# A trunk layer in float32: the input projection by one level of Strassen, its result kept in DRAM

## The chip, the cores and the metric

The kernel runs on one NeuronCore of a Trainium2 chip. The metric is the device time of one execution in microseconds (us). The engines of the core work side by side, each through its own list of instructions in a fixed order: TensorE (PE; PEld is its loading of weights), VectorE (DVE), ScalarE (ACT), GpSimd (POOL) and SyncE (SP), which here issues DMAs. A tile is a buffer in SBUF; a bank is 512 float32 columns of PSUM, where matmuls put their results.

## The reference

```python
u = rms_norm(h, ln_g[i])                         # 1024 tokens x 1024
z = u @ w_in[i]                                  # 1024 x 7168
c_val, c_glu, c_gate, hq, hf, hi, hg = jnp.split(z, split_pts, axis=-1)
y_conv = conformer_conv_branch(c_val, c_glu, c_gate, ...)   # causal conv of 31 taps, LayerNorm, @ w_pw2
y_hgrn = hgrn2_branch(hq, hf, hi, hg, lbs[i], onorm_g[i])   # 8 heads, gated recurrence in chunks
h = h + concatenate([y_conv, y_hgrn]) @ w_out[i]            # 2048 x 1024
gate = sigmoid(rms_norm(h, pe_norm_g[i]) @ w_pg[i])
h = h + gate * (p[i] @ w_pp[i])
return rms_norm(h, final_g)
```

All of it is float32; the five large products are those with w_in, w_pw2, w_out, w_pg and w_pp.

## The kernel before

Every float32 operand of a large product is split exactly into a high and a low float32r part, and a product is three matmuls: high by high, high by low, low by high. `split` makes the parts: ScalarE copies the high one (L113), VectorE subtracts (L114). `prep` loads a weight block of 512 KB into one of three raw buffers of pool `wp` and splits it there.

First x is scaled by its RMS (`scale_x`), transposed and split into `uh`, `ul` (`norm_x`), each half of the tokens by itself; the projection of p (the layer embedding) is computed and put into DRAM. Then follows the z phase. `ztile` takes one block of 128 columns of w_in and gives two PSUM banks with 512 tokens each, by 48 matmuls of 512 columns (L241 to L243). `values` gives two blocks of the heads' values with tokens on partitions, by 192 matmuls of 256 columns (L263 to L265). The activations read z straight out of PSUM. ORDER says in which order the projections of head and channel group h, its convolution (C) and its recurrent head (H) are written; the scheduler of the language then orders each engine's list by priorities. A convolution is 29 taps of 128x1024 on VectorE (L452) and a LayerNorm through transposes. The last eight z tiles, of the convolution's gate, are written behind all heads (`conv_gate`).

After that come `pw` (w_pw2; 8 tiles of 48 matmuls, the gate read back from DRAM), the output projection with tokens on partitions, its first four token blocks in `oA` (all 16 row blocks of w_out in one go, with the heads' results `yhr` loaded and split between them) and the other four in `oB`, then `norm_T` and the gated layer embedding `pg` (w_pg) with the last RMSNorm.

Of the kernel before, what the change touches and what calls it, by code (L numbers as in the profile page):

```python
# [123 lines left out]

# [605 lines left out]
```

## Time and profile before

| | us |
|---|---|
| three runs, median (lowest to highest) | 1146.06 (1145.87 to 1147.56) |
| span of the profiled execution, 0.44 above that median | 1146.5 |
| PE busy | 1124.8 |
| DVE busy | 739.5 |
| ACT busy | 443.0 |
| POOL busy | 72.0 |
| first z matmul starts | 49.1 |
| first pw matmul starts | 781.7 |

An engine is busy while one of its instructions runs. Matmuls overlap, so a matmul's cost is the distance from its start to the next one's. In a timeline a row's bracket gives the idle time before it and what ended that.

### The profile page before, as it was taken

What the parts mean: (1) busy time and instruction counts of PE and PEld (TensorE: products, weight loads), DVE (VectorE), ACT (ScalarE), POOL (GpSimd) and SP (SyncE); (2) the same over time, 40 slices, a digit from 0 to 9 for tenths busy, and PEclk for the clock granted to TensorE, in tenths of its full rate; (3) what the DMA queues carried; (4) which work ended last, traced back from release to release, by engine and by line L of the source; (5) the groups of instructions that cost most, each with busy time, mean ns of one, the idle gap of its engine ahead of it and who ended that gap; (6) DMA issues with size and microseconds to landing.
All of it is one profiled execution on the core that took longest, in us unless ns stands there. A gap on an engine that the chain in (4) does not pass through costs nothing.

```text
span 1146.5 us, 17744 instructions
## 1 busy us (share of the span) xinstructions
PE 1124.8 (98%) x7408; PEld 945.6 (82%) x7408; DVE 739.5 (65%) x1145; ACT 443.0 (39%) x811; POOL 72.0 (6%) x107
## 2 busy tenths in 40 slices
PE   6999999999999999999999999999999999999997
PEld 4888978889888789788898788888888888887886
DVE  3659579998499996599993896242334325226444
ACT  4823244253354442344532632442123324126333
POOL 3100001001001010010010010000000001001000
PEclk9899999999999999999999999999999999999999
DMA  7611121211111112111111112277335632334221
GB/s 247 236 37 55 37 66 30 74 55 39 55 57 56 59 35 74 56 37 56 57 56 56 57 56 93 74 242 254 110 92 165 195 99 77 107 109 149 92 92 56
DMA packets 85715, 104.60 MB, mean 91 GB/s; under 512 B 3290, under 2 KB 65754, under 8 KB 85634
## 3 DMA queue, kind: packets, MB, share of 16 engines
q1 hardware_dynamic: 85634, 103.46, 28.1%
q8 instruction: 58, 0.95, 0.3%
q14 instruction: 23, 0.19, 0.1%
HBM read 82.48 MB, written 20.97 MB: 90 GB/s over the span
## 4 chain that ended last, share of the span: by engine, by line
PE 89%; DVE 6%; DMA 2%; ACT 1%; issue 1%; SPq 0%; POOL 0%; POOLq 0%; ACTq 0%
PE z L241 14%; PE z L242 14%; PE z L243 14%; DVE y L452 4%; PE v L264 3%; PE v L265 3%; PE v L263 3%; PE pg L683 3%; PE pg L684 3%; PE pg L682 3%; PE oA L591 3%; PE pw L243 3%; PE pw L241 3%; PE oA L589 3%; PE oA L588 3%; PE pw L242 3%
## 5 line engine op out<-in xcount | busy, mean ns | idle before, releaser
L452 DVE SCALAR_TENSOR_TENSOR y<-vpad,par,y 128x1024 f32<-128x1024 f32 x232 | 288.8, 1278 | 1.1
L682 PE MATMUL pg<-gh,hh 128*128 128x512 f32 (+1 forms) x136 | 51.4, 378 | 0.0
L683 PE MATMUL pg<-gl,hh 128*128 128x512 f32 (+1 forms) x136 | 51.4, 378 | 0.0
L684 PE MATMUL pg<-gh,hl 128*128 128x512 f32 (+1 forms) x136 | 51.3, 377 | 0.0
L519 DVE TENSOR_TENSOR vpad<-z,gl 128x512 f32<-128x512 f32 x16 | 11.0, 691 | 42.7 <-PE z L243 42.7
L263 PE MATMUL v<-wv_0h,uh 128*128 128x256 f32 x128 | 36.7, 287 | 0.0
L265 PE MATMUL v<-wv_0h,ul 128*128 128x256 f32 x128 | 36.5, 285 | 0.0
L264 PE MATMUL v<-wv_0l,uh 128*128 128x256 f32 x128 | 36.5, 285 | 0.0
L263 PE MATMUL v<-wv_1h,uh 128*128 128x256 f32 x128 | 36.2, 283 | 0.0
L264 PE MATMUL v<-wv_1l,uh 128*128 128x256 f32 x128 | 36.2, 283 | 0.0
L265 PE MATMUL v<-wv_1h,ul 128*128 128x256 f32 x128 | 36.2, 283 | 0.0
L266 ACT ACTIVATE vt<-v 128x256 f32<-128x256 f32 x32 | 12.2, 382 | 58.9 <-PE v L265 58.9
L688 DVE TENSOR_TENSOR gt<-gt,pet 128x512 f32<-128x512 f32 (+1 forms) x17 | 11.2, 661 | 36.1 <-ACT gt L687 36.1
L108 POOL TENSOR_SCALAR ro<-sso 128x8 f32<-128x8 f32 x8 | 8.4, 1054 | 389.9 <-ACT on L129 389.9
L475 DVE TENSOR_SCALAR y<-yt,mv,ry 128x128 f32<-128x128 f32 x64 | 23.5, 404 | 13.1 <-POOL ry L109 13.1
L570 DVE SCALAR_TENSOR_TENSOR sgr<-pw,par,sgr 128x512 f32<-128x512 f32 x16 | 12.0, 750 | 30.1 <-PE pw L243 30.1
L437 ACT ACTIVATE on<-o,ro 128x128 f32<-128x128 f32 x64 | 18.5, 386 | 29.0 <-POOL ro L109 29.0
L682 PEld LDWEIGHTS pg<-gh,hh 128*128 128x128 f32 x136 | 25.6, 188 | 4.7
L683 PEld LDWEIGHTS pg<-gl,hh 128*128 128x128 f32 x136 | 25.6, 188 | 4.7
L684 PEld LDWEIGHTS pg<-gh,hl 128*128 128x128 f32 x136 | 25.6, 188 | 4.5
L483 ACT ACTIVATE yc<-yn,par 128x512 f32<-128x512 f32 x16 | 12.5, 778 | 39.8 <-PE yn L482 39.8
L129 ACT ACTIVATE on<-o 128x128 f32<-128x128 f32 x64 | 16.9, 278 | 23.3 <-PE up L409 18.9
(802 smaller groups left out, 3463.6 us busy)
## 6 DMA issues: line engine op xcount, KB each, us to landing
wz<-in_w_in_dram SPq DMA_DIRECT2D x48, 512.0 KB
wo<-in_w_out_dram SPq DMA_DIRECT2D x32, 512.0 KB
xt<-in_x_dram SPq DMA_DIRECT2D x8, 512.0 KB
pe_d<-pes SPq DMA_DIRECT2D x8, 512.0 KB
wv<-in_w_in_dram SPq DMA_DIRECT2D x8, 512.0 KB
yc_d<-yc SPq DMA_DIRECT2D x8, 512.0 KB
yh_d<-sgT SPq DMA_DIRECT2D x8, 512.0 KB
sg_d<-sgc SPq DMA_DIRECT2D x8, 512.0 KB
```

Of the source, the lines that this page charges most:

```text
L241: mm(z, lhsT=wh[:, k, :], rhs=mh[hf][k], start=k == 0, stop=False)
L242: mm(z, lhsT=wh[:, k, :], rhs=ml[hf][k], start=False, stop=False)
L243: mm(z, lhsT=wl[:, k, :], rhs=mh[hf][k], start=False, stop=k == G - 1)
L263: mm(z, lhsT=uh[hf][k][:, c], rhs=wh, start=k == 0, stop=False)
L264: mm(z, lhsT=uh[hf][k][:, c], rhs=wl, start=False, stop=False)
L265: mm(z, lhsT=ul[hf][k][:, c], rhs=wh, start=False, stop=k == G - 1)
L452: nc.vector.scalar_tensor_tensor(y[j % 2], vp[:, j:j + T], pcol(g, j), y[j % 2], op0=ALU.mult, op1=ALU.add)
L588: mm(z, lhsT=mixh[hf][k][:, c], rhs=wh[j], start=first, stop=False)
L589: mm(z, lhsT=mixh[hf][k][:, c], rhs=wl[j], start=False, stop=False)
L682: mm(z, lhsT=hh[k][:, c], rhs=gh[j][k][:, o:o + w], start=k == 0, stop=False)
L683: mm(z, lhsT=hh[k][:, c], rhs=gl_[j][k][:, o:o + w], start=False, stop=False)
L684: mm(z, lhsT=hl[k][:, c], rhs=gh[j][k][:, o:o + w], start=False, stop=k == G - 1)
```

## The change

The product of the normalised input and w_in is computed by one level of Strassen's algorithm in Winograd's form. The 56 column tiles of z are taken in 28 pairs (`zpair`). The input is cut into four quarters a, b, c, d (halves of its channels by halves of the tokens), and the seven operands a, c, d and t1 to t4 are made once, from all of x (`norm_x`, `quarter`). The weights of a pair are cut into four quarters of 256 KB, four sums of them are made on VectorE, and each of the seven factors is split: ScalarE writes the negated high part into the low tile and the high part into its own, and a DMA issued by GpSimd adds the source to the low tile in place (`factor`), where VectorE subtracted. A product is 12 matmuls of 512 columns, a pair 84. Partial sums leave PSUM by copies on ScalarE and additions on VectorE, and the four quarters of z go to DRAM; `ztile` reads a column tile back when it is needed. The values are now transposed on TensorE (`head`). The normalisation in the convolution moves from VectorE to ScalarE. In the output projection `project` takes all eight token blocks through the convolution's half of w_out, then the heads' results are loaded, and then all through the other half; each half adds to the residual by itself. Pool `wp` has two buffers instead of three.

```diff
+C_VAL, C_GLU, C_GATE, H_Q, H_F, H_V, H_G = range(7)
+RAWS, TMPS = 6, 6
+AHEAD, SOON = 3000, 4000
+ORDER = "cCCcCh" + "HCHcCh" * 2 + "HCHhHH" + "gggg"
...
+        def quarter(name, k, src, sign=1.0):
+            nc.scalar.activation(xh[name][k], src, AF.Copy, scale=sign)
+            h = xh[name][k].bitcast(F32)
+            if sign == 1.0:
+                nc.vector.tensor_tensor(xl[name][k], src, h, op=ALU.subtract)
+            else:
+                nc.vector.scalar_tensor_tensor(xl[name][k], src, sign, h,
+                                               op0=ALU.mult, op1=ALU.subtract)
+        def norm_x(k):
+            q = {}
+            for n, kk, hf in (("a", k, 0), ("c", k + KH, 0), ("b", k, 1), ("d", k + KH, 1)):
+                pt = bank("t", f"u{n}{k}")
                 for b in range(4):
-                    nc.tensor.transpose(pt[:, b * P:(b + 1) * P], xs[b][:, k * P:(k + 1) * P],
-                                        ident)
-                uh[hf][k] = up.tile([P, H], F32R, tag="u", name=f"uh{hf}_{k}")
-                ul[hf][k] = up.tile([P, H], F32R, tag="u", name=f"ul{hf}_{k}")
-                nc.scalar.activation(uh[hf][k], pt, AF.Copy, scale=pcol(k, R_LN))
-                nc.vector.scalar_tensor_tensor(ul[hf][k], pt, pcol(k, R_LN),
-                                               uh[hf][k].bitcast(F32),
-                                               op0=ALU.mult, op1=ALU.subtract)
-        xs = scale_x(0)
+                    nc.tensor.transpose(pt[:, b * P:(b + 1) * P],
+                                        xs[hf * 4 + b][:, kk * P:(kk + 1) * P], ident)
+                q[n] = st.tile([P, H], F32, tag=f"uf{n}", name=f"uf{n}{k}")
+                nc.scalar.activation(q[n], pt, AF.Copy, scale=pcol(kk, R_LN))
+                if n != "b":
+                    quarter(n, k, q[n])
+            a, b, c, d = (q[n] for n in "abcd")
+            nc.vector.tensor_tensor(a, a, b, op=ALU.subtract)
+            quarter("t1", k, a)
+            nc.vector.tensor_tensor(a, a, d, op=ALU.add)
+            quarter("t2", k, a, -1.0)
+            nc.vector.tensor_tensor(b, d, b, op=ALU.subtract)
+            quarter("t3", k, b)
+            nc.vector.tensor_tensor(c, a, c, op=ALU.subtract)
+            quarter("t4", k, c)
...
+        scale_x(1)
+        layer_embedding(1)
+        for k in range(KH):
+            norm_x(k)
...
+        def factor(name, src):
+            hi = wq.tile([P, KH, P], F32R, tag="hi", name=f"w{idx}_{name}h")
+            lo = wq.tile([P, KH, P], F32R, tag="lo", name=f"w{idx}_{name}l")
+            nc.scalar.activation(lo, src, AF.Copy, scale=-1.0)
+            nc.scalar.activation(hi, src, AF.Copy)
+            nc.gpsimd.dma_start(out=lo, in_=src, accum_op=ALU.add)
+            return hi, lo
+        def add(name, x, y):
+            o = raw(name)
+            nc.vector.tensor_tensor(o, x, y, op=ALU.add)
+            return o
+        w = {}
+        for name, r, c in (("11", 0, 0), ("21", 0, 1), ("22", 1, 1), ("12", 1, 0)):
+            w[name] = raw(name)
+            nc.sync.dma_start(w[name], w_in[r * H:(r + 1) * H, (idx + c) * P:(idx + c + 1) * P]
+                              .rearrange("(k p) c -> p k c", p=P))
+        s1 = add("s1", w["21"], w["22"])
+        s2 = add("s2", s1, w["11"])
+        s4 = add("s4", s2, w["12"])
+        s3 = add("s3", w["11"], w["21"])
+        return [factor(n, t) for n, t in (("f1", w["11"]), ("f5", s1), ("f6", s2), ("f3", s4),
+                                          ("f7", s3), ("f2", w["12"]), ("f4", w["22"]))]
+    def zpair(proj, i):
+        idx = proj * G + 2 * i
+        with tc.high_priority(AHEAD):
+            fs = weights(idx)
+        def product(z, f, xn, first, last):
+            wh, wl = f
+            for k in range(KH):
+                mm(z, lhsT=wh[:, k, :], rhs=xh[xn][k], start=first and k == 0, stop=False,
+                   skip_group_check=True)
+                mm(z, lhsT=wh[:, k, :], rhs=xl[xn][k], start=False, stop=False,
+                   skip_group_check=True)
+                mm(z, lhsT=wl[:, k, :], rhs=xh[xn][k], start=False, stop=k == KH - 1,
+                   skip_group_check=True)
+        def tmp(name):
+            return wq.tile([P, H], F32, tag="tmp", bufs=TMPS, name=f"z{idx}_{name}")
+        def copy(z, name, scale=1.0):
+            t = tmp(name)
+            with tc.high_priority(SOON):
+                nc.scalar.activation(t, z, AF.Copy, scale=scale)
+            return t
+        def out(t, c, hf):
+            nc.sync.dma_start(z_d[idx + c][:, hf * H:(hf + 1) * H], t)
+        f1, f5, f6, f3, f7, f2, f4 = fs
+        za, zd, zb = bank("za", f"za{idx}"), bank("zd", f"zd{idx}"), bank("zb", f"zb{idx}")
+        product(za, f1, "a", True, False)
+        m1 = copy(za, "m1")
+        product(zd, f5, "t1", True, False)
+        p5 = copy(zd, "p5")
+        product(za, f6, "t2", False, False)
+        u2 = copy(za, "u2")
+        product(zd, f3, "d", False, True)
+        with tc.high_priority(SOON):
+            nc.vector.tensor_tensor(u2, u2, zd, op=ALU.add)
+        out(u2, 0, 1)
+        product(za, f7, "t3", False, False)
+        u3 = copy(za, "u3")
+        with tc.high_priority(SOON):
+            nc.vector.scalar_tensor_tensor(u3, u3, -1.0, p5, op0=ALU.mult, op1=ALU.subtract)
+        out(u3, 1, 1)
+        product(zb, f2, "c", True, True)
+        with tc.high_priority(SOON):
+            nc.vector.tensor_tensor(m1, m1, zb, op=ALU.add)
+        out(m1, 0, 0)
+        product(za, f4, "t4", False, True)
+        out(copy(za, "c21", -1.0), 1, 0)
...
+    def ztile(proj, m):
+        t = wk.tile([P, T], F32, tag="ld", bufs=3, name=f"ld{proj}_{m}")
+        nc.sync.dma_start(t, z_d[proj * G + m])
+        return t
...
             r = rstd_of(mv[:, :, 1], G, 1.0, f"ry{g}")
+            nmr = sml.tile([P, G], F32, tag="nmr", name=f"nmr{g}")
+            nc.gpsimd.tensor_scalar(nmr, mv[:, :, 0], -1.0, 0.0, op0=ALU.mult, op1=ALU.add)
+            nc.gpsimd.tensor_tensor(nmr, nmr, r, op=ALU.mult)
...
+        zv = ztile(H_V, h)
+        vt = wk.tile([P, G, P], F32, tag="vt", name=f"vt{h}")
+        for hf in range(2):
+            pt = bank("t", f"v{h}_{hf}")
+            for c in range(4):
+                cc = hf * 4 + c
+                nc.tensor.transpose(pt[:, c * P:(c + 1) * P], zv[:, cc * P:(cc + 1) * P], ident)
+            nc.scalar.activation(vt[:, hf * 4:hf * 4 + 4, :],
+                                 pt.rearrange("p (c v) -> p c v", c=4), AF.Copy)
...
+    zx.close()
+    pz = ctx.enter_context(tc.tile_pool(name="pz2", bufs=1, space=PSUM, reuse_waits="tile"))
+    wp = ctx.enter_context(tc.tile_pool(name="wp", bufs=2, reuse_waits="tile"))
+    up = ctx.enter_context(tc.tile_pool(name="up2", bufs=32, reuse_waits="tile"))
     yp = ctx.enter_context(tc.tile_pool(name="yp", bufs=32, reuse_waits="tile"))
...
-        nc.sync.dma_start(sg, sg_d[m])
+        nc.sync.dma_start(sg, z_d[C_GATE * G + m])
+        nc.scalar.activation(sg, sg, AF.Silu)
...
+    def project(src_h, src_l, row0, hf, j, flip):
+        zs = [bank("z", f"o{row0}_{hf}_{j}_{b}") for b in range(4)]
+        kks = range(G // 2)[::-1 if flip else 1]
+        for n, kk in enumerate(kks):
+            wh, wl = prep(w_out[row0 + kk * 2 * P:row0 + (kk + 1) * 2 * P, j * H:(j + 1) * H]
+                          .rearrange("(k p) c -> p k c", p=P), [P, 2, H], f"wo{row0}_{hf}_{j}_{kk}")
+            for i in range(2):
+                k = 2 * kk + i
+                first, last = n == 0 and i == 0, n == G // 2 - 1 and i == 1
+                for b, z in enumerate(zs):
+                    c = slice(b * P, (b + 1) * P)
+                    mm(z, lhsT=src_h[hf][k][:, c], rhs=wh[:, i, :], start=first, stop=False)
+                    mm(z, lhsT=src_h[hf][k][:, c], rhs=wl[:, i, :], start=False, stop=False)
+                    mm(z, lhsT=src_l[hf][k][:, c], rhs=wh[:, i, :], start=False, stop=last)
+        for b, z in enumerate(zs):
+            h = halves(hs[hf * 4 + b])[j]
+            nc.vector.tensor_tensor(h, z, h, op=ALU.add)
+    for hf in range(2):
         for j in range(2):
-            zs[b, j] = bank("zt"[j], f"oA{b}_{j}")
-    def prep_out(k):
-        return prep(w_out[k * P:(k + 1) * P, :], [P, D], f"wo{k}")
-    ws = [prep_out(k) for k in range(3)]
-    for k in range(2 * G):
-        if k < G:
-            load_split(yh_d[k], mhh, mhl, k, f"yhr{k}")
...
+    for j in range(2):
+        project(mhh, mhl, D, 0, j, False)
...
+        project(mhh, mhl, D, 1, j, j == 1)
```

**VectorE's list, where z ends.** In the kernel before, the rows from the last taps of convolution 7 to the split of its result `ycl`; `wz22`, `wz23` are weights of the gate's tiles, `sgT` a head's result, L303 begins head 7.

```order
L452 SCALAR_TENSOR_TENSOR y_7_6315<-vpad_600,par,y_7_6315 128x1024
L452 SCALAR_TENSOR_TENSOR y_7_6316<-vpad_600,par,y_7_6316 128x1024
L452 SCALAR_TENSOR_TENSOR y_7_6315<-vpad_600,par,y_7_6315 128x1024
L303 TENSOR_TENSOR QD_6018<-QD_6018,F_6016 128x32x16
L454 TENSOR_TENSOR y_7_6315<-y_7_6315,y_7_6316 128x1024
...
L114 TENSOR_TENSOR wz22l<-wz_7024,wz22h 128x1024
L443 SCALAR_TENSOR_TENSOR sgT_6019<-ot_0_6646,par,sgT_6019 128x512
L114 TENSOR_TENSOR wz23l<-wz_7084,wz23h 128x1024
L443 SCALAR_TENSOR_TENSOR sgT_6019<-ot_1_6656,par,sgT_6019 128x512
L114 TENSOR_TENSOR ycl_0_7151<-ycr_7182,ych_0_7150 128x512
```

In the changed kernel, from the last additions of pair 28 (L348, L352) on: `vpad` is the input of convolution 7, L549 its taps, L394 begins head 5.

```order
L348 SCALAR_TENSOR_TENSOR z_u_8201<-z_u_8201,z_p_8159 128x512
L352 TENSOR_TENSOR z_m_8145<-z_m_8145,zb_8132 128x512
L505 SCALAR_TENSOR_TENSOR S_5945<-S_5945,F_128_5942,up_0_5958 128x128 x3
L544 TENSOR_TENSOR vpad<-ld_7_6030,ld_7_6028 128x1024
L549 SCALAR_TENSOR_TENSOR y_7_6034<-vpad,par,y_7_6034 128x1024
...
L549 SCALAR_TENSOR_TENSOR y_7_6034<-vpad,par,y_7_6034 128x1024
L394 TENSOR_TENSOR QD_6133<-QD_6133,F_6126 128x32x16
L551 TENSOR_TENSOR y_7_6034<-y_7_6034,y_7_6035 128x1024
L563 BN_STATS bs_0_6074<-yt_0_6069 128x6 x2
...
L124 TENSOR_TENSOR ycl_0_8253<-ycr_8284,ych_0_8252 128x512
```

The taps of convolution 7 stood ahead of the last gate weights; now they stand behind the last addition of z, and head 5 with them.

**TensorE's list, from the last z matmul to the first of pw.** Before:

```order
L242 MATMUL z_1_7115<-ul_7_586,wz23h 128x512
L243 MATMUL z_1_7115<-uh_7_585,wz23l 128x512
L241 MATMUL pw_0_7270<-ych_0_7150,wpw0h 128x512
L242 MATMUL pw_0_7270<-ycl_0_7151,wpw0h 128x512
L243 MATMUL pw_0_7270<-ych_0_7150,wpw0l 128x512
```

In the changed kernel (L318 is z; `yt`, `yn` are convolution 7's transposes, `sc`, `up`, `o` and `ot` steps of heads 4 to 6, `v` the values' transposes):

```order
L318 MATMUL za_8130<-t4h_185,w_f4l 128x512
L535 MATMUL ot_0_6011<-ident,on_5974 128x128 x4
L559 MATMUL yt_0_6069<-ident,y_7_6034 128x128 x4
L581 MATMUL yn_0_6107<-ident,y_7_6035 128x128 x4
L604 MATMUL v_0_6139<-ident,ld_5_6136 128x128 x4
L386 MATMUL sc_1_6152<-QD_6133,K_6127 32x48 x32
...
L500 MATMUL up_1_6353<-vt_6138,kt_6330 128x128
L500 MATMUL up_0_6344<-vt_6138,kt_6330 128x128
...
L535 MATMUL ot_0_6397<-ident,on_6360 128x128 x4
L386 MATMUL sc_1_7062<-QD_7043,K_7037 32x48 x32
L386 MATMUL sc_8_7153<-Q_8_7141,K_7037 32x48 x32
L646 MATMUL pw_0_8373<-ych_0_8252,wpw0h 128x512
```

Nothing stood between z and pw; now convolution 7's transposes, head 5 and the scores of head 6 do.

**SP's list, at the loads of the heads' results.** Before, `yhr` and the weights `wo` alternate:

```order
L556 DMA yhr_8064<-yh_d_95 128x1024
L119 DMA wo_8094<-in_w_out_dram 128x1024
L556 DMA yhr_8100<-yh_d_96 128x1024
L119 DMA wo_8130<-in_w_out_dram 128x1024
L119 DMA wo_8160<-in_w_out_dram 128x1024
L119 DMA wo_8190<-in_w_out_dram 128x1024
```

In the changed kernel, from the end of the first pass (`wo_1_1_...`) to the start of the second (`wo_0_0_...`):

```order
L634 DMA wo_1_1_1_9350<-in_w_out_dram 128x2x512
L634 DMA wo_1_1_2_9380<-in_w_out_dram 128x2x512
L634 DMA wo_1_1_3_9410<-in_w_out_dram 128x2x512
L663 DMA yhr_9444<-yh_d_140 128x1024
L663 DMA yhr_9450<-yh_d_141 128x1024
L663 DMA yhr_9456<-yh_d_142 128x1024
...
L663 DMA yhr_9486<-yh_d_147 128x1024
L634 DMA wo_0_0_0_9496<-in_w_out_dram 128x2x512
L634 DMA wo_0_0_1_9526<-in_w_out_dram 128x2x512
```

All eight `yhr` loads now stand together, ahead of the second pass's first weight block.

## Rows read from the trace of the kernel before

**Rows 1.** The page: busy time by engine, and VectorE's busy tenths in 40 slices

```profile
PE 1124.8 (98%) x7408; PEld 945.6 (82%) x7408; DVE 739.5 (65%) x1145; ACT 443.0 (39%) x811; POOL 72.0 (6%) x107
...
DVE  3659579998499996599993896242334325226444
```

**Rows 2.** Windows: us, busy us and (instructions) of PE, PEld, DVE, ACT, POOL; clock, DMA

```profile
0.00:49.10 49.10, 37.31 (x168) 30.46 (x169) 24.56 (x41) 31.16 (x54) 16.96 (x43) 0.93 0.75 250
92.00:781.70 689.70, 688.03 (x5420) 583.31 (x5420) 538.63 (x869) 277.15 (x541) 43.18 (x32) 1.00 0.21 67
781.70:868.80 87.10, 87.10 (x386) 72.15 (x385) 32.14 (x41) 18.97 (x27) 0.00 (x0) 1.00 0.41 132
500.00:600.00 100.00, 99.76 (x763) 84.83 (x762) 96.46 (x144) 41.78 (x95) 9.42 (x6) 1.00 0.17 54
```

**Rows 3.** Timeline of PE, first z tiles: start us, us, instruction, count

```profile
47.71 1.64 PE L171 MATMUL ut<-ident,xt 128*128 128x128 f32 x13 [1.05 <-DVE xt L162]
49.11 0.47 PE L241 MATMUL z<-uh,wz8h 128*128 128x512 f32 x1
...
61.90 0.39 PE L241 MATMUL z<-uh,wz0h 128*128 128x512 f32 x1
...
72.78 0.39 PE L241 MATMUL z<-uh,wz32h 128*128 128x512 f32 x1
```

**Rows 4.** Windows of line L241 alone, one of the three lines of z's matmuls

```profile
61.70:92.00 30.30, 17.30 (x45) 8.42 (x45) 1.00 0.18 52
92.00:781.70 689.70, 283.19 (x708) 133.11 (x708) 1.00 0.21 67
```

**Rows 5.** Timeline of PE, first `values` set: its first matmul and what follows it

```profile
105.42 0.28 PE L263 MATMUL v<-wv_0h,uh 128*128 128x256 f32 x1
...
128.45 1.04 PE L462 MATMUL yt<-ident,y 128*128 128x128 f32 x8
```

**Rows 6.** Tile xt: the scaling of x, count, min/median/max ns, first and last start

```profile
L162 DVE TENSOR_SCALAR xt<-xt,rx x8: 753/754/2686, 15.3 to 45.0; 128x1024 f32<-128x1024 f32 x8
```

**Rows 7.** Timeline of ACT, operations of 512 columns one behind the other

```profile
30.26 0.67 ACT L175 ACTIVATE uh<-ut,par 128x512 fp32r<-128x512 f32 x1
30.83 0.59 ACT L231 ACTIVATE pes<-pe 128x512 f32<-128x512 f32 x1
31.30 0.69 ACT L175 ACTIVATE uh<-ut,par 128x512 fp32r<-128x512 f32 x1
```

**Rows 8.** Groups by form: count, busy us, mean ns of one, idle time before

```profile
L109 POOL TENSOR_TENSOR ro<-ro,mhalf 128x8 f32<-128x8 f32 x8 | 19.5, 2439 | 0.7
...
L449 ACT ACTIVATE y<-vpad,par 128x1024 f32<-128x1024 f32 x8 | 10.0, 1246 | 0.0
...
L108 POOL TENSOR_SCALAR ro<-sso 128x8 f32<-128x8 f32 x8 | 8.4, 1054 | 389.9 <-ACT on L129 389.9
```

**Rows 9.** Timeline of DVE from the last taps to pw

```profile
670.38 8.45 DVE L452 SCALAR_TENSOR_TENSOR y<-vpad,par,y 128x1024 f32<-128x1024 f32 x7
...
682.67 3.67 DVE L452 SCALAR_TENSOR_TENSOR y<-vpad,par,y 128x1024 f32<-128x1024 f32 x3
686.26 0.68 DVE L303 TENSOR_TENSOR QD<-QD,F 128x512 f32<-128x512 f32 x1
...
729.64 0.35 DVE L414 SCALAR_TENSOR_TENSOR S<-S,F,up 128x128 f32<-128x128 f32 x1 [0.58 <-PE up L409]
...
755.90 3.70 DVE L114 TENSOR_TENSOR ycl<-ycr,ych 128x512 fp32r<-128x512 f32 x6 [4.39 <-ACT ych L113]
...
775.89 1.23 DVE L114 TENSOR_TENSOR wpw0l<-wpw,wpw0h 128x1024 fp32r<-128x1024 f32 x1 [2.12 <-ACT wpw0h L113]
```

**Rows 10.** Chain that ended last, at the end of oB: start us, us, what

```profile
1033.87 4.44 DMA wpg<-in_w_pg_dram
1038.33 0.64 ACT gh L113
1039.00 1.30 DVE gl L114 x2
1040.32 4.59 DMA wpg<-in_w_pg_dram
```

**Rows 11.** Tile rx: GpSimd's one-column multiply

```profile
L109 POOL TENSOR_TENSOR rx<-rx,mhalf x8: 550/550/555, 14.7 to 44.4; 128x1 f32<-128x1 f32 x8
```

**Rows 12.** The page: DMA queue, packets, MB, share of 16 engines

```profile
q1 hardware_dynamic: 85634, 103.46, 28.1%
```

More of the change, by code (lines that the diff above doesn't have):

```diff
@@ L76, in load_params @@
     def load_params(work):
-        rows = work.tile([NR, D], F32, name="prow")
+        rows = work.tile([NR, D], F32, tag="xt", bufs=8, name="prow")
         nc.sync.dma_start(rows[0:TAPS, :], conv_w[0])
@@ L181, in trunk_kernel @@
+        xs = []
+        layer_embedding(0)
+        scale_x(0)
         load_params(st)
@@ L274, in trunk_kernel @@
+    wk = ctx.enter_context(tc.tile_pool(name="wk", bufs=1, side="right", reuse_waits="tile"))
+    AT = wk.tile([P, G, P], F32, name="AT")
+    nc.gpsimd.memset(AT, 0.0)
     AB = wk.tile([P, G, 32], F32, name="AB")
     nc.gpsimd.memset(AB, 0.0)
-    vpads = [wk.tile([P, PAD + T], F32, name=f"vpad{i}") for i in range(2)]
-    for i in range(2):
-        nc.gpsimd.memset(vpads[i][:, :PAD], 0.0)
-    def hgrn(h, QD, K, F, vt, sgT):
-        A, B = AT[h % 2], AB
+    vp = wk.tile([P, PAD + T], F32, tag="vpad", name="vpad")
@@ new lines, in trunk_kernel @@
+    groups, heads, pairs = iter(range(G)), iter(range(G)), {k: iter(range(G // 2)) for k in "chg"}
+    for step in ORDER:
+        if step == "C":
+            conv(next(groups))
+        elif step == "H":
+            head(next(heads))
+        else:
+            i = next(pairs[step])
+            for proj in {"c": (C_GLU, C_VAL), "h": (H_F, H_Q, H_V, H_G), "g": (C_GATE,)}[step]:
+                zpair(proj, i)
+    zx.close()
+    pz = ctx.enter_context(tc.tile_pool(name="pz2", bufs=1, space=PSUM, reuse_waits="tile"))
@@ L545, in half_tiles, with product @@
+    def product(wh, wl, mh, ml, tag, name):
+        res = []
+        for hf in range(2):
+            z = bank(tag, f"{name}_{hf}")
+            for k in range(G):
+                mm(z, lhsT=wh[:, k, :], rhs=mh[hf][k], start=k == 0, stop=False)
+                mm(z, lhsT=wh[:, k, :], rhs=ml[hf][k], start=False, stop=False)
+                mm(z, lhsT=wl[:, k, :], rhs=mh[hf][k], start=False, stop=k == G - 1)
+            res.append(z)
+        return res
     def half_tiles(pool, tag, name):
@@ L573, in trunk_kernel @@
     mhh, mhl = half_tiles(yp, "y", "mh")
-    mixh = [mch[i] + mhh[i] for i in range(2)]
-    mixl = [mcl[i] + mhl[i] for i in range(2)]
-    hs = [hp.tile([P, D], F32, name=f"h{tb}") for tb in range(G)]
+    hs = []
     for tb in range(G):
-        nc.sync.dma_start(hs[tb], x[tb * P:(tb + 1) * P, :])
-    def accumulate(zs, hf, k, wh, wl, first, last):
-        for b in range(4):
-            c = slice(b * P, (b + 1) * P)
-            cols = [(j, z) for (bb, j), z in zs.items() if bb == b]
-            for j, z in cols:
-                mm(z, lhsT=mixh[hf][k][:, c], rhs=wh[j], start=first, stop=False)
-                mm(z, lhsT=mixh[hf][k][:, c], rhs=wl[j], start=False, stop=False)
-            for j, z in cols:
-                mm(z, lhsT=mixl[hf][k][:, c], rhs=wh[j], start=False, stop=last)
@@ L617, in trunk_kernel @@
+    for hf in range(2):
+        for j in range(2):
+            project(mch, mcl, 0, hf, j, False)
+    for k in range(G):
+        load_split(yh_d[k], mhh, mhl, k, f"yhr{k}")
     rs = [None] * G
```

242 lines of the change are left out of this document (92 added, 150 removed).

## The prediction, made before the changed kernel was run

> **What bounds the kernel now.** I read the page first. TensorE is busy for 1124.8 of 1146.5 us and VectorE for 739.5 [rows 1]; in the slices VectorE is near its limit only in the middle, and in 500 to 600 us both are (99.8 and 96.5 us of 100) [rows 2]. The busy time of matmuls is modelled, so I looked next at whether TensorE waits: from 92 us to the first pw product at 781.7 it is idle for 1.7 us of 689.7, and in pw not at all [rows 2]. So TensorE's instruction list is the bound from about 49 us, where the first z matmul starts [rows 3], to nearly the end, and a matmul taken away is worth its distance to the next one, if nothing else becomes late. That distance is (72.78 - 61.90) / 48 = 0.2267 us for 512 columns [rows 3]. One `values` set is 192 matmuls of 256 columns from 105.42 to 128.45 us, 0.120 each [rows 5].
>
> From 92 to 781.7 us stand 3 x 708 = 2124 matmuls of 512 columns [rows 4] (481 us) and four `values` sets (92). What is left of the 688 busy us, 115 us, is the small work of eight heads and eight convolutions. A transpose is 1.40 / 13 = 0.108 us [rows 3]; the 128 of the convolutions take 14 us, so a head takes TensorE about 12.6 us.
>
> **What the change saves.** z was 48 x 48 = 2304 matmuls of 512 columns and 768 of 256: 522 + 92 = 614 us. Strassen has 28 pairs x 84 = 2352 of 512: 533 us. That is 81 us less; the values now need 64 transposes (7 us). Net -74 us. I now go through the stages to see how much of it is kept.
>
> **First pair.** Before, 48 + 135 z matmuls were done at 92 us: the first tile from 49 to 61.7, then 45 on each of three lines [rows 3, 4]. Now all seven quarter combinations need all eight x blocks, and the first pair cannot end before the last combination. The last x block is scaled at 45 us [rows 6]; in the new order the second layer embedding (48 matmuls, 10.9 us) goes ahead of the first transpose of x, whose start I therefore put at 53 us. From there ScalarE has 54 operations of 512 columns to the last combination; back to back such ones follow at 0.47 to 0.57 us [rows 7], so 29 us, to 82; then the VectorE subtraction behind the last, the fourth-block matmuls that wait for it, and small waits in the chain of each block. I take 92 us for the end of pair 1 (between 85 and 100). Before had 183 matmuls done by then, now 84: 22 us lost.
>
> **Pairs 2 to 28.** 27 x 84 x 0.2267 = 514 us, and the small work that the new TensorE order has inside them: all but the fifth head's end, the last convolution's transposes and three heads, so 115 - 3.2 x 12.6 - 1.8 = 73, with 4 for the values' transposes 77. Last z matmul at 92 + 514 + 77 = 683, if no pair waits. For the waits I have three prices. ScalarE must copy four of seven partial sums out of PSUM, each within one product (12 x 0.2267 = 2.72 us); a copy costs about 0.6 [rows 7], but the convolution's scalings of 1024 columns (1.25 each) [rows 8] can stand ahead of it. VectorE loses the weight subtractions and gains 4 + 3 adds a pair, about what it loses, and each pair's share stays under 20 us. The accumulating DMA has no row at all; it is a rival below. Lower bound of the waits 0, upper 100 us; I take 11, a stall of 0.4 us a pair, near the end where the copies fit.
>
> **Between the last z matmul and pw.** Before, conv and head 7 ended under the gate tiles wz16 to wz23: the last taps at 686.3, the head's last state at 730, the splits of yc from 756 [rows 9], all while TensorE computed z. Now the gate's four pairs are on TensorE before the last convolution: VectorE's order has the whole of conv 7 behind the last z addition, and of heads 5 and 6 what stands before the first pw matmul. That list, at distances between starts: 31 operations of 1024 columns on conv 7, 29 of them taps at 8.45 / 7 = 1.207 us [rows 9], with its statistics 39 us; head 5 and half of head 6, where a head is about 17.7 us (head 7's operations from 686.26 to 751 added up, without their waits) 29 us with the rest of head 4; 16 splits at 3.70 / 6 = 0.62, and one weight, 11 us [rows 9]. Together 79; less what may run under the last product, 76 us. TensorE has some 19 us of small work there and waits for 57. First pw matmul at 683 + 11 + 76 = 770. Its cover gone, each microsecond of this list is one of the time; I see no lower price than the rows, an upper one if PE and VectorE alternate in heads 5 and 6 (+15).
>
> **From pw to the end.** It took 1146.5 - 781.7 = 364.8 us. Added: the rest of head 6 and head 7 on TensorE, 1.5 x (12.6 + 0.9) = 20. The 16 more residual additions lie on an idle VectorE (32 of 87 us busy in pw) [rows 2]: nothing, or 0.7 each at the four pass ends if not. Between the passes all eight loads of yh stand on SP ahead of the first block of the second pass, through two raw buffers instead of three and no longer one by one between the blocks. One turn of a buffer is 4.44 + 0.64 + 1.30 = 6.4 us [rows 10], so two buffers give one load per 3.2 us; nine are 29 us, of which the last two blocks of the first pass (24 matmuls each, 5.4 us) hide 11: 18 us (10 to 22). The same for the eight loads of w_pg, which already now wait for such turns at the end of oB [rows 10]: 9 us more (5 to 13), since products start as parts arrive.
>
> **Sum.** 92 + 514 + 77 + 11 + 76 + 365 + 20 + 27 = 1182; I say **1180 us**. It stands against this execution's span of 1146.5, 0.4 above the median of the three times. The gain on TensorE is real and smaller than what its waits give back (22 + 11 + 57 + 27 = 117 against 74).
>
> **Rival 1: faster.** The mechanism is the gap before pw. It costs 57 us of waiting because I took VectorE's written order as what happens. For it: TensorE's own list still is 74 us shorter, and before it hid everything for 700 us. Against it: the engine cannot pass the rows, and 35 us of them are taps with a firm price. It decides at 57 - 36 = 21 us of waiting; with 10 us there, and half the other stalls, 1182 - 47 - 30 = 1105. Chance 0.30, and 0.03 for a time within 0.2%, which is about what a measurement of this kernel can tell from no change.
>
> **Rival 2: the accumulating DMA bounds z.** Each of 196 lower parts now goes ScalarE, GpSimd issue, a DMA that reads two operands, and the landing, in place of one VectorE subtraction of 1.3 us. The factor buffers are five for seven factors a pair, the raw buffers six for seven. Two chained turns of this path and about three product steps make a pair's period, so the path may take about (19 - 3 x 2.72) / 2 = 5.4 us unseen. The nearest row is 4.44 us for a plain load of 512 KB [rows 10], 256 KB is half, and reading twice puts it back: 4.4 plus 1.2 for two ScalarE operations and the issue, right at that limit. At 8 us the period is 24 and not 19: 27 x 4 to 5 gives about 1285. GpSimd's queue speaks for it too: its wait for heads is 390 us [rows 8], an accumulate behind such a waiting instruction waits along, and its 8-column multiply took 2.44 us [rows 8] where a 1-column one had 0.55 [rows 11]. Then the bytes: q1's 103.46 MB took 28.1% of 16 engines' span [rows 12], that is 322 us; z's loads, accumulates, stores and reads are 144 MB or 447 us, 607 with the accumulates read twice, in a stretch of 590 us. The Trainium skill, DMA: Bandwidth & Descriptors, Anatomy of one DMA, gives 2.0 us plus bytes at 436 GB/s for a DMA from GpSimd; by that 256 KB would be an estimated 2.6 us, no wait, and the sum 1170. No run here shows it. Its page SBUF — State Buffer, Who interferes with whom, says that VectorE instructions with two SBUF inputs contend with GpSimd instructions that read SBUF; the slow multiply agrees, though a descriptor is written, not read. Chance of this rival 0.22, time 1215 to 1330.
>
> **Forecast's own case.** 0.45, range 1150 to 1215. That leaves faster 0.30, same 0.03, slower 0.67. The range that holds 8 in 10 reaches into both rivals: 1105 to 1275.
>
> **What would show it.** After: 28 pairs at 19 us or, with a head between, 23 to 26; a gap on TensorE of 50 to 60 us right before the first pw product with VectorE full of taps; first pair's end near 92 us; a wait of some 18 us between the passes, ended by DMA of yhr or wo. Wrong if pairs wait for the lower weight parts (then GpSimd or its DMAs stand ahead of L318 in the waits), if the gap before pw is under 25 us, or if VectorE or ScalarE keeps TensorE waiting in every pair.

## The result, and the profile after

The changed kernel takes 1341.47 us (median of 4 runs, 1339.59 to 1348.92) against 1146.51 before: ratio 1.1705, 95% interval 1.1671 to 1.1738. It is slower by 17%, and outside the predicted range of 1105 to 1275. The page of the profiled execution, with the lines that answer to [rows 1] and [rows 12]:

```profile
span 1337.9 us, 18528 instructions
PE 1116.2 (83%) x6752; PEld 898.1 (67%) x6752; DVE 803.8 (60%) x1267; ACT 688.4 (51%) x1323; POOL 233.4 (17%) x317
...
DVE  3282685788757845965965876857633334344644
...
PEclk8679998999899999999999997576899999899999
...
q1 hardware_dynamic: 116002, 153.81, 34.2%
q0 software_dynamic: 28224, 51.39, 22.2%
```

TensorE's busy time has hardly fallen, although z has fewer matmul columns: some of its rows are longer (up to 796 ns in the rows below, where the median is 389), and it is idle for a sixth of the span. By line, one row each for the first and last starts of the first and of the seventh product of a pair, and of the first pw tile:

```profile
L314 PE MATMUL za<-ah,w_f1h x112: 387/389/796, 69.8 to 781.2; 128*128 128x512 f32 x112
...
L314 PE MATMUL za<-t4h,w_f4h x112: 388/389/628, 110.1 to 812.2; 128*128 128x512 f32 x112
```

```profile
L646 PE MATMUL pw<-ych,wpw0h x16: 387/391/796, 921.1 to 941.6; 128*128 128x512 f32 x16
```

So pair 1's last product starts at 110.1 us, pair 28's last product starts the last of these matmuls at 812.2, and pw begins at 921.1. These marks lie within 2 us of the ends of products that the prediction names. The windows of z, of the gap before pw, of pw and of the output projection (columns as in [rows 2]):

```profile
112.80:812.20 699.40, 623.66 (x3900) 499.15 (x3899) 484.76 (x742) 419.54 (x802) 186.26 (x222) 0.97 0.75 185
812.20:921.10 108.90, 36.12 (x549) 29.23 (x547) 79.83 (x140) 50.60 (x112) 6.23 (x8) 0.59 0.34 119
921.10:1041.40 120.30, 114.31 (x804) 94.15 (x801) 58.24 (x105) 53.13 (x110) 3.67 (x4) 0.96 0.37 124
1041.40:1239.70 198.30, 182.98 (x818) 150.80 (x817) 80.50 (x100) 56.31 (x80) 2.98 (x8) 0.96 0.35 115
```

| | predicted | measured |
|---|---|---|
| last product of pair 1 starts | 92, less 2.7 | 110.1 |
| from there to pair 28's | 602 (591 of work, 11 of waits) | 702.1 |
| gap before pw | 76 | 108.9 |
| pw to the end | 412 | 416.8 |

Nearly two thirds of the error are in z. VectorE's longest wait there, and two of TensorE's (us in total, times, longest):

```profile
DVE w_s L290 <- DMA w_f2l<-w: 74.4, 22, 10.9
...
PE yt L559 <- DVE y L551: 23.8, 7, 4.0
...
PE za L314 <- ACT z_u L327: 13.0, 10, 3.3
```

No row says that TensorE waits for a low weight part. It waits for the convolutions' ends, for copies out of PSUM and for steps of the heads. The chain that ended last (the work that the end of the kernel followed from, step by step) shows how such a wait begins (start, us, what):

```profile
345.14 5.54 DMA w_f2l<-w
...
350.76 0.69 DVE w_s L290
351.45 1.15 DVE y L551
352.64 1.97 PE yt L559 x8
...
357.44 0.86 POOL w_f5l L285
```

The accumulating DMA of one factor holds a raw buffer. VectorE's next weight sum L290 needs that buffer, and the convolution's last addition L551 stands behind the sum in VectorE's list; the transposes `yt`, which TensorE's list has in the middle of a pair, wait for that. (The last row is the issue of such a DMA on GpSimd, 0.86 us.) In TensorE's timeline the distance from a z matmul to its next instruction, less 0.2267 us, adds up to 87 us between 112.8 and 814 over the matmuls whose excess is above 0.3 us; 25 of them stand ahead of `yt`. Where nothing holds a pair it needs what was counted, 19.1 us from its first matmul to the next pair's:

```profile
318.80 0.39 PE L314 MATMUL za<-ah,w_f1h 128*128 128x512 f32 x1
...
337.88 0.39 PE L314 MATMUL za<-ah,w_f1h 128*128 128x512 f32 x1
```

Of the eleven pairs without a convolution or head on TensorE, four took 19.0 to 19.5 us and seven 20.4 to 24.0. Pair 2 (23.4 us) shows that a wait costs more than its length. Its rows, and the window behind the wait:

```profile
123.44 0.39 PE L318 MATMUL zd<-dh,w_f3l 128*128 128x512 f32 x1
126.35 0.79 PE L314 MATMUL za<-t3h,w_f7h 128*128 128x512 f32 x1 [2.52 <-ACT z_u L327]
126.94 0.63 PE L316 MATMUL za<-t3l,w_f7h 128*128 128x512 f32 x1
127.37 0.63 PE L318 MATMUL za<-t3h,w_f7l 128*128 128x512 f32 x1
...
129.50 0.42 PE L316 MATMUL za<-t3l,w_f7h 128*128 128x512 f32 x1
129.76 0.40 PE L318 MATMUL za<-t3h,w_f7l 128*128 128x512 f32 x1
```

```profile
126.30:129.50 3.20, 3.15 (x7) 2.48 (x8) 1.29 (x2) 2.07 (x4) 1.63 (x2) 0.50 0.27 50
```

After 2.5 us without work the granted clock is 0.50 for 3.2 us, the lower of TensorE's two levels (1.2 of 2.4 GHz), and matmuls follow at 0.43 us and not 0.2267: the eight before 129.76 take 3.4 us and not 1.8. Over z TensorE is idle for 76 us (699.4 less 623.7 busy); the other third of the 111 us by which z exceeds its count is not idle time but work that took longer than counted.

### The profile page after: what moved, and what is told of

The parts are those of the page before. It is cut to its first block, busy times and chain, and to the rows that moved or that the text cites. A ratio compares the mean times of both kernels' runs of the same rounds, so it can differ in the third digit from the quotient of the medians.

```text
span 1337.9 us, 18528 instructions
## 1 busy us (share of the span) xinstructions
PE 1116.2 (83%) x6752; PEld 898.1 (67%) x6752; DVE 803.8 (60%) x1267; ACT 688.4 (51%) x1323; POOL 233.4 (17%) x317
## 3 DMA queue, kind: packets, MB, share of 16 engines
q0 software_dynamic: 28224, 51.39, 22.2%
## 4 chain that ended last, share of the span: by engine, by line
PE 45%; DVE 17%; DMA 15%; issue 12%; ACT 6%; POOL 4%; SPq 0%; POOLq 0%; DVEq 0%; ACTq 0%
DMA w_f2l<-w 7%; DVE y L549 6%; PE o L708 4%; PE o L709 4%; PE o L710 4%; PE za L314 3%; PE za L316 3%; PE za L318 3%; DVE w_s L290 2%; PE pg L781 2%; PE pg L782 2%; PE pg L780 2%; PE pw L646 2%; PE pw L647 2%; PE pw L648 2%
## 5 line engine op out<-in xcount | busy, mean ns | idle before, releaser
L549 DVE SCALAR_TENSOR_TENSOR y<-vpad,par,y 128x1024 f32<-128x1024 f32 x232 | 285.5, 1279 | 12.2 <-ACT y L546 8.5
L290 DVE TENSOR_TENSOR w_s<-w,w 128x512 f32<-128x512 f32 x56 | 38.8, 693 | 94.4 <-DMA w_f2l<-w 75.4
L290 DVE TENSOR_TENSOR w_s<-w_s,w 128x512 f32<-128x512 f32 x56 | 38.5, 688 | 56.8 <-DMA w_f5l<-w_s 27.6
L314 PE MATMUL za<-t3h,w_f7h 128*128 128x512 f32 x112 | 47.1, 420 | 9.3 <-ACT z_u L327 9.3
L314 PE MATMUL za<-ah,w_f1h 128*128 128x512 f32 x112 | 45.7, 408 | 9.0 <-ACT ah L197 9.0
L314 PE MATMUL za<-t2h,w_f6h 128*128 128x512 f32 x112 | 46.1, 412 | 5.8 <-ACT z_m L327 5.8
L314 PE MATMUL za<-t4h,w_f4h 128*128 128x512 f32 x112 | 45.9, 410 | 3.7 <-ACT z_u L327 3.7
L314 PE MATMUL zd<-t1h,w_f5h 128*128 128x512 f32 x112 | 46.0, 411 | 1.0 <-ACT t1h L197 1.0
L316 PE MATMUL zd<-t1l,w_f5h 128*128 128x512 f32 x112 | 45.6, 407 | 1.3 <-DVE t1l L200 1.3
L318 PE MATMUL za<-t4h,w_f4l 128*128 128x512 f32 x112 | 46.0, 411 | 0.0
L316 PE MATMUL za<-t3l,w_f7h 128*128 128x512 f32 x112 | 45.9, 410 | 0.0
L316 PE MATMUL za<-al,w_f1h 128*128 128x512 f32 x112 | 45.9, 409 | 0.0
L318 PE MATMUL za<-t3h,w_f7l 128*128 128x512 f32 x112 | 45.6, 407 | 0.0
```

What stands on the lines that cost most here:

```text
L290: nc.vector.tensor_tensor(o, x, y, op=ALU.add)
L314: mm(z, lhsT=wh[:, k, :], rhs=xh[xn][k], start=first and k == 0, stop=False, skip_group_check=True)
L316: mm(z, lhsT=wh[:, k, :], rhs=xl[xn][k], start=False, stop=False, skip_group_check=True)
L318: mm(z, lhsT=wl[:, k, :], rhs=xh[xn][k], start=False, stop=k == KH - 1, skip_group_check=True)
L549: nc.vector.scalar_tensor_tensor(y[j % 2], vp[:, j:j + T], pcol(g, j), y[j % 2], op0=ALU.mult, op1=ALU.add)
```

## The experiments

Stages of all runs, in us: the start of pair 1's last product; from there to pair 28's; the gap before pw; from pw to the end; the time (the profiled span is the sum of the four).

| run | first | z | gap | rest | time |
|---|---|---|---|---|---|
| changed kernel | 110.1 | 702.1 | 108.9 | 416.8 | 1341.5 |
| e1 DMA copies, doesn't add | 106.2 | 659.2 | 107.8 | 415.6 | 1290.5 |
| e2 DMA of 8 KB | 109.2 | 650.2 | 99.3 | 415.1 | 1275.6 |
| e3 no DMA | 100.0 | 624.6 | 97.4 | 415.9 | 1239.7 |
| e4 VectorE subtracts | 98.5 | 596.6 | 196.5 | 438.6 | 1331.9 |
| e5 convolution 7 short | 109.8 | 705.4 | 78.5 | 416.0 | 1311.4 |
| e6 embedding later | 105.5 | 710.3 | 107.8 | 415.8 | 1338.3 |
| e7 GpSimd subtracts | 108.7 | 793.0 | 88.2 | 414.8 | 1406.5 |
| e8 seven raw buffers | 111.2 | 701.9 | 108.4 | 414.7 | 1335.5 |
| e9 gate held back | 109.4 | 828.5 | 62.0 | 387.9 | 1384.6 |
| e10 four partial sum buffers | 111.7 | 705.7 | 109.1 | 415.7 | 1343.9 |
| e11 six factor buffers | 113.3 | 708.0 | 99.6 | 415.0 | 1337.6 |
| e12 DMAs on other tiles | 101.7 | 772.0 | 107.3 | 414.8 | 1397.9 |
| e13 DMAs that nobody waits for | 103.6 | 643.1 | 115.9 | 415.8 | 1280.1 |

Runs e1 to e5, e7 and e10 to e13 were executed once; four executions of one kernel lie 5 to 11 us apart, so that smaller differences between single runs say nothing.

Theory A: the lower part's way through ScalarE, GpSimd and a DMA makes z long. Theory B: the lists of the engines are in lockstep (each waits in turn for the other's next step) whatever the DMA does.

**e1, the add.**

```diff
-            nc.gpsimd.dma_start(out=lo, in_=src, accum_op=ALU.add)
+            nc.gpsimd.dma_start(out=lo, in_=src)
```

> The DMA of each lower part copies its source (with the cast) instead of adding to the low tile; the low parts are wrong, every list of instructions is the same as in the changed kernel. Theory A (the way of the lower part through ScalarE, GpSimd and a DMA holds the raw buffers, and VectorE and all behind it wait): if the second read of the add is the price, the median landing falls by over 1 us from 3.2 to 5.5 and the time by 30 to 80 us, to 1260 to 1310; if it is the fixed part of the way, landing and time stay, 1325 to 1345. Theory B (the lists themselves are in lockstep: copies out of PSUM and steps of heads and convolutions stand too early): 1335 to 1345.

1290.5 us; z fell by 43. The landings (last number, median us from issue to arrival) and the engines' time on GpSimd's queue q0, of the changed kernel first:

```profile
w_f1l<-w POOLq DMA_DIRECT2D x28, 256.0 KB, 4.1
...
w_f6l<-w_s POOLq DMA_DIRECT2D x28, 256.0 KB, 3.2
...
w_f2l<-w POOLq DMA_DIRECT2D x28, 256.0 KB, 5.5
```

Then of e1:

```profile
q0 software_dynamic: 28224, 51.39, 12.7%
...
w_f1l<-w POOLq DMA_DIRECT2D x28, 256.0 KB, 2.3
...
w_f2l<-w POOLq DMA_DIRECT2D x28, 256.0 KB, 4.3
```

The same 51.39 MB took 12.7% of 16 engines over 1288.8 us, 164 us, and with the add 22.2% of 1337.9, 297 us: 1.8 times. By the medians of the seven factors the add's share of the way is 0.7 to 2.5 us.

**e2 and e3, what else the way costs.**

```diff
-            nc.gpsimd.dma_start(out=lo, in_=src, accum_op=ALU.add)
+            nc.gpsimd.dma_start(out=lo[:, 0, 0:16], in_=src[:, 0, 0:16], accum_op=ALU.add)
```

> Each lower part's DMA adds only 16 of 512 columns (8 KB instead of 256); the low parts are wrong. The issue on GpSimd and the fixed part of the landing stay, the bytes go (51 MB twice read). Theory A by bytes: 1240 to 1290, landings of about 2 us. Theory A by the fixed part: 1310 to 1340. Theory B: 1330 to 1345.

e3 has no such line at all.

> The DMA of the lower parts is left out; the low parts stay the negated high ones, so the result is wrong. Nothing but the two ScalarE operations and the matmuls holds a raw buffer. Theory A: pairs 2 to 28 fall from 702 us to 600 to 640, the whole to 1235 to 1280. Theory B: the whole stays above 1320, since lists, copies and PSUM banks are the same.

1275.6 and 1239.7. Of z's 702 us the add takes 43, the other bytes 9 (within the noise), and the issue with what a landing of 8 KB still takes (2.0 to 4.3 us) 26: 77 in all, with 10 at the start and 11 in the gap. Theory B is out as the main cause. In e3 VectorE's largest wait for a weight sum and TensorE's for the convolutions are

```profile
DVE w_s L289 <- ACT w_f2l L283: 23.3, 8, 6.2
...
PE yt L558 <- DVE y L550: 1.1, 1, 1.1
```

and the sum over TensorE's timeline, made as above, is 21 us for 87. What is left of z's 625 beyond the 591 counted is not the DMA's; that it is theory B's lockstep is not shown.

**e4, VectorE again.**

```diff
-            nc.scalar.activation(lo, src, AF.Copy, scale=-1.0)
             nc.scalar.activation(hi, src, AF.Copy)
-            nc.gpsimd.dma_start(out=lo, in_=src, accum_op=ALU.add)
+            nc.vector.tensor_tensor(lo, src, hi.bitcast(F32), op=ALU.subtract)
```

> The lower parts of the 196 factors are made by VectorE's subtraction again (0.69 us each, 135 us in z), the DMA and one of two ScalarE operations go. The result is the reference's. Theory A: the raw buffers come free after 1.3 us and not 5 to 8, which is worth more than VectorE's 135 us as VectorE has some 200 us free in z: 1260 to 1310. Theory B: VectorE's list grows, its steps for heads and convolutions come later and TensorE waits longer: 1360 to 1420.

1331.9, neither of the two. z takes 597 us, 5 from the 602 predicted, and TensorE is through with it 117 us earlier; but pw starts only 30 us earlier:

```profile
101.20:695.10 593.90, 573.08 (x3271) 468.55 (x3270) 510.00 (x767) 290.03 (x534) 22.55 (x26) 0.99 0.38 124
695.10:891.60 196.50, 63.70 (x917) 51.00 (x915) 149.61 (x263) 72.15 (x154) 11.51 (x16) 0.58 0.25 89
```

VectorE's work is not done, and the gap of 196 us takes the gain: it is VectorE's list that says when pw can start (e9 below). From pw on this run is 22 us longer than the changed kernel, as more of the heads' steps stand behind pw's start.

**e5, the gap.**

```diff
-        for j in range(2, TAPS):
+        for j in range(2, TAPS if g < G - 1 else 3):
```

> Convolution 7 alone leaves out 28 of its 31 taps on VectorE (28 x 1.207 = 34 us); its result is wrong. If VectorE's written list between the last z addition and pw is what TensorE waits for, the gap before pw falls by 30 to 36 us from 109 and the time to 1300 to 1312. If the gap is set by the chain of heads 5 and 6 through TensorE, ScalarE and GpSimd, or by the loads and splits of yc, it falls by less than 15 and the time stays above 1325.

1311.4; the gap fell by 30.4 of the 34 us of taps left out. VectorE's list sets it. That list, from the input of convolution 7 to the weight of pw:

```profile
816.36 1.23 DVE L544 TENSOR_TENSOR vpad<-ld,ld 128x1024 f32<-128x1024 f32 x1 [3.03 <-DMA ld<-z_d]
821.21 34.77 DVE L549 SCALAR_TENSOR_TENSOR y<-vpad,par,y 128x1024 f32<-128x1024 f32 x29 [3.62 <-ACT y L546]
...
870.96 0.69 DVE L124 TENSOR_TENSOR ycl<-ycr,ych 128x512 fp32r<-128x512 f32 x1 [5.54 <-ACT ych L123]
...
903.20 0.75 DVE L537 SCALAR_TENSOR_TENSOR ld<-ot,par,ld 128x512 f32<-128x512 f32 x1 [6.13 <-PE ot L535]
...
908.71 0.69 DVE L394 TENSOR_TENSOR QD<-QD,F 128x512 f32<-128x512 f32 x1 [3.13 <-ACT QD L597]
...
920.94 1.22 DVE L124 TENSOR_TENSOR wpw0l<-wpw,wpw0h 128x1024 fp32r<-128x1024 f32 x1
```

VectorE is busy for 79.8 of the 108.9 us (the window above), the 79 of the prediction; the other 29 are its waits for ScalarE, TensorE and loads, which the list's sum hasn't.

**e6, the start.** `layer_embedding(1)` is written behind the loop over `norm_x`.

> The second layer embedding is written behind the preparation of the quarters instead of ahead of it. If its place ahead of the first transpose of x is part of the late start, the first transposes move from 62.5 us to about 50 and the end of the first pair and the time by 8 to 14 us, ratio 0.990 to 0.994 to the changed kernel's 1341. If the start is bound by ScalarE's conversions or by the loads of x, under 3 us.

1338.3 (1336.3 to 1341.2; ratio to before 1.166, 1.1641 to 1.1679): the first transposes of x start at 43.2 us and not 62.5, pair 1's last product only 4.6 us earlier, and z gives that back. The time lies within the spread of the changed kernel's: the embedding's place isn't what costs here.

**e7, GpSimd itself.**

```diff
-            nc.scalar.activation(lo, src, AF.Copy, scale=-1.0)
-            nc.gpsimd.dma_start(out=lo, in_=src, accum_op=ALU.add)
+            nc.gpsimd.tensor_tensor(lo, src, hi.bitcast(F32), op=ALU.subtract)
```

> The lower parts are subtracted by GpSimd itself (128x512, two operands in SBUF), with no DMA and one ScalarE operation per factor less; the result is the reference's. No row shows such an operation; one of 8 columns took 1.7 to 2.4 us. If it takes under 2.7 us (a seventh of a pair), raw buffers come free early and z goes like the run without accumulation, 600 to 640 us, the whole 1230 to 1270. If it takes 4 us or more, GpSimd is the bound of each pair (28 us): 1400 and more.

The operation takes 1.5 to 1.8 us (medians), under the limit of 2.7, and yet z grew by 91 us: a miss. Groups by form (between the bars busy us and the mean ns of one):

```profile
L548 DVE SCALAR_TENSOR_TENSOR y<-vpad,par,y 128x1024 f32<-128x1024 f32 x232 | 387.3, 1717 | 7.4 <-ACT y L545 5.6 <-ACT y L546 1.7
...
L284 POOL TENSOR_TENSOR w_f4l<-w,w_f4h 128x512 fp32r<-128x512 f32 x28 | 50.1, 1790 | 41.4 <-ACT w_f4h L283 37.5 <-PE zd L317 3.9
```

VectorE's taps took 1717 ns where they took 1279: beside GpSimd's subtractions they are a third slower. The Trainium skill, SBUF — State Buffer, Who interferes with whom, says that VectorE instructions with two SBUF inputs contend with GpSimd instructions that read SBUF. The trace agrees (1717 and 1279 ns). Of the slow multiply that the prediction takes for a sign of it, part is this and part its size: before, the 8-column multiply took 2.55 us beside the taps and 1.64 with VectorE idle, the 1-column one 0.55.

**e8, e10, e11: buffers.** RAWS, TMPS = 7, 5; 6, 4; and 6, 4 with six buffers for each part of a factor.

> Seven raw buffers of 256 KB for the weights instead of six, five buffers for partial sums instead of six. Theory A (raw buffers held by the lower part's DMA make VectorE's sums wait): pairs 2 to 28 fall by 15 to 50 us from 702, the time to 1290 to 1326. If the factor buffers (five for seven factors) or the copies out of PSUM hold the pair instead: within 8 us of 1341, or slower by the missing partial sum buffer.

> Control for e8 and e11: four buffers for partial sums instead of six, nothing else; the lists are the same. If these buffers are not waited for: 1335 to 1350. If they are (and so hid a gain of the seventh raw buffer in e8): 1355 and more.

> Six buffers each for high and low parts instead of five, four for partial sums. If ScalarE's wait for a factor buffer, held until its product ends, is what carries the DMA's delay on to everything behind it: pairs 2 to 28 fall by 20 to 50 us from 702, the time to 1290 to 1325 (against e10). If not: within 10 us of e10.

1335.5 (1331.7 to 1343.1; ratio to before 1.165, 1.1608 to 1.1692), 1343.9 and 1337.6; z is 702, 706 and 708. The control (e10) costs nothing, so the other two can be read: neither a seventh raw buffer nor a sixth factor buffer shortens z. In e8 the wait has only moved to another factor, and TensorE's wait for the convolutions has grown:

```profile
DVE w_s L290 <- DMA w_f7l<-w_s: 46.1, 11, 9.5
...
PE yt L559 <- DVE y L551: 33.2, 7, 6.1
...
DVE w_s L290 <- DMA w_f2l<-w: 14.5, 11, 3.0
```

So the raw buffer in the chain above is where the delay was seen, not a limit whose end would cure it.

**e9, the lost cover.** A one-column copy from convolution 6 (gate pairs 1, 2) or 7 (3, 4) into the raw buffers, ahead of their loads.

```diff
+            if idx // G == C_GATE:
+                nc.vector.tensor_copy(w[name][:, 0, 0:1], mk[6 + idx % G // 4])
             nc.sync.dma_start(w[name], w_in[r * H:(r + 1) * H, (idx + c) * P:(idx + c + 1) * P]
```

> The four pairs of the gate are held back by a one-column write into their raw buffers: pairs 1 and 2 until convolution 6 has its taps, 3 and 4 until convolution 7 has. The result is the reference's. If the gap is lost cover (TensorE's z work done too early, while VectorE's list sets when pw can start), the other 24 pairs end some 100 us earlier, VectorE reaches conv 7 30 to 60 us earlier, the gap before pw falls under 50 and the time to 1280 to 1312. If VectorE's list as a whole is the bound from the first convolution to pw, whatever TensorE does beside it, the time stays within 12 us of 1341.

1384.6 (ratio to before 1.2066, 1.2046 to 1.2086), a miss of both: the gap is 62 us, but VectorE did not reach convolution 7 earlier, and the held pairs then came late. The four pairs stand last on TensorE in the changed kernel too, so that the other 24 had nothing to gain: the 24th makes its last addition on VectorE at 701 us there and at 708 here. The input of convolution 7 is the last start of this row, of e9 first, then of e4:

```profile
L548 DVE TENSOR_TENSOR vpad<-ld,ld x8: 1218/1226/1228, 148.4 to 819.6; 128x1024 f32<-128x1024 f32 x8
```

```profile
L543 DVE TENSOR_TENSOR vpad<-ld,ld x8: 1217/1224/1226, 128.6 to 822.6; 128x1024 f32<-128x1024 f32 x8
```

In the changed kernel it is 816.4. So with the last z matmuls at 812, 938 and 695 us, VectorE comes to convolution 7 at 816 to 823. In e9 it comes there with the last additions of three pairs still to make, and no earlier: its own list and waits set that time, the end of z does not. (In e4 that list is another, with the subtractions and without the DMA's waits; that its time is so near is chance.) Without the accumulates, in e3, it is 718.5: what the lower part's way holds up is VectorE's list.

**e12 and e13, load or length.** e12 lets GpSimd add between two tiles that nobody reads.

> As e3 (no DMA on the lower parts, which stay wrong), but GpSimd issues in the same place an accumulating DMA of the same 256 KB between two tiles that nobody waits for; four buffers for partial sums, which e10 shows to cost nothing. If the DMA engines' load by the accumulates slows the other transfers and so z: back to 1310 to 1345. If it is the length of the lower part's own way, which work waits for: 1240 to 1275, near e3's 1240 or e2's 1276.

1397.9, above both ranges and inconclusive: the DMAs waited for nothing but each other, and the convolution's small steps on GpSimd stood behind rows of them:

```profile
POOL dmy L291 <- DMA dmy<-ah: 229.0, 163, 4.8
...
ACT y L581 <- POOL nmr L575: 145.2, 6, 61.7
```

e13 binds them to the pair's time.

```diff
-            nc.gpsimd.dma_start(out=lo, in_=src, accum_op=ALU.add)
+            for i in range(2):
+                nc.gpsimd.dma_start(out=dpl.tile([P, KH, P], F32, name=f"scr{idx}_{name}{i}"), in_=hi.bitcast(F32))
```

> As e3 (no DMA on the lower parts, which stay wrong), but behind each high part GpSimd issues two plain DMAs of that high part, 256 KB each, into DRAM that nobody reads: about the accumulates' share of the DMA engines, held to the pair's own time, and nothing of the pair waits for them except a high part's buffer, which its product holds longer. If the engines' load (and two issues of 0.86 us) is what made z long: z 690 to 720 us, the whole 1320 to 1350. If it is the length of the lower part's own way: z 625 to 650, the whole 1240 to 1275.

z is 643 us with the DMA engines as busy as in the changed kernel (0.77 and 0.75) and moving more:

```profile
106.30:746.70 640.40, 604.75 (x3859) 490.03 (x3858) 482.84 (x735) 418.13 (x798) 225.10 (x406) 0.98 0.77 277
```

That is within the range for the length of the way (625 to 650); the whole, 1280.1, is a little above its range of 1240 to 1275. Against e3 the load and two issues a factor cost 18 us in z and 40 in the whole, 18 of these in the gap. By subtraction the other 59 of the 77 in z, and 60 of the 100 in the whole, are the length of the lower part's own way. This holds as far as two plain copies into DRAM load the engines as one accumulate within SBUF does, which no run separates.

## Why the prediction was wrong

- **What TensorE saves:** right where nothing holds it: a z matmul has its 0.2267 us, a pair 19.1. Behind waits the matmuls ran at 0.43 us, a cost that the prediction has nowhere.
- **First pair:** 92 was 113. The first transposes came at 62.5 us and not 53, and ScalarE's 54 operations from there took 39 us (63.6 to 102.5) where 29 were counted back to back: it waits 7.5 us between them, for VectorE above all, and one takes 0.58 us and not 0.54. e3 gives 10 us of the 21 to the accumulating DMA (its transposes come at 54.2); e6 shows that the embedding's place isn't the rest.
- **Waits in pairs 2 to 28: the step that failed.** "Lower bound of the waits 0, upper 100 us; I take 11": they were 111 (702 less 591). The forecast's own case took the copies out of PSUM for the limit and gave the lower part's way no cost; taking that way's DMA out gives 77 of the 111 back (e3). So the likeliest case was the wrong one, and rival 2 came true. Its price (27 x 4 to 5) met the waits, but not by its arithmetic, and its time (1215 to 1330) was too low, as the first pair and the gap came on top. It had every pair at 24 us by five factor and six raw buffers; pairs 2 and 3 took that, but others 19, one buffer more of either kind changed nothing, and the load of its bytes counts for 18 us in z at most. The way of 5 to 8 us (issue 0.86, landing 3.2 to 5.5, two ScalarE operations) stands where a VectorE subtraction of this size takes 0.69 us (e4; the prediction's 1.3 is one of twice the columns), and every list that waits for it once can make the next list wait, as the chain shows. The sign that the prediction named, GpSimd or its DMAs ahead of L318 in the waits, did not appear: the delay reaches TensorE through VectorE and ScalarE.
- **The estimate from the Trainium skill** of 2.6 us for 256 KB from GpSimd (DMA: Bandwidth & Descriptors, Anatomy of one DMA): a copy with a cast landed in 2.3 to 4.3 us, near it at the low end; with the add it took 3.2 to 5.5, so the figure of a plain transfer was the wrong one to set beside it.
- **Gap before pw:** the list was right (79.8 us busy for 79), its waits (29 us, where 15 stood as an upper bound) were left out. That the gap follows the end of z was wrong: e4 and e9 show VectorE's list as its own bound, and in the changed kernel the two only fall near each other (812 and 816 us). Rival 1 needed TensorE to wait 21 us or less there; it waited 73 (108.9 less 36.1 busy).
- **After pw:** 412 was 417, so near by luck, as errors of both signs cancel. The loads of yh stopped TensorE once, for 15.3 us where 18 were counted, and at the place that the prediction named:

```profile
1143.93 1.22 PE L708 MATMUL o<-wo_0h,mhh 128*128 128x512 f32 x2 [15.28 <-ACT wo_0h L123]
```

  w_pg cost nothing (9 counted); pw with the end of heads 6 and 7 took 120 us where 107 were counted.
- **The sum:** its check, 117 us given back against 74 gained, would make 1190 and not the stages' 1182; the two were never brought together, which matters little here.

Through which buffer or list the length of the way acts first is not settled; one more buffer of either kind was tried, more of both at once was not.

## What to carry to other kernels

Before an operation is moved from a busy engine to a DMA, compare the whole way (issue, landing, the read of both operands) with the operation that it replaces, and list what stands behind each engine that waits for a buffer on that way; a saving on the bound engine is kept only if all lists that feed it keep pace. Where a second engine is busy for three quarters of a phase, sum its own list to the phase's end as a bound of its own, with its waits, instead of adding it behind the first engine's. An engine's recorded wait shows where a delay surfaces; take the suspect away before a buffer is added for it.

## What the runs showed that was not expected

An accumulating DMA kept the DMA engines 1.8 times as long as a copy of the same bytes (297 and 164 us). GpSimd's subtraction of 128x512 (1.5 to 1.8 us) made VectorE's taps beside it a third slower (1717 and 1279 ns). TensorE's granted clock was 0.59 over the gap before pw, and 0.97 over z with its many short waits, where it was 1.00 before [rows 2]; after one wait of 2.5 us it was 0.50 for 3.2 us, which cost another 1.6 us.
